# A two-layer decoder trunk on one core: early products, weight sums by DMA and one shared pool

## The chip, the cores and the metric

The kernel runs on one core of a Trainium2 chip. A core has TensorE (PE, matmuls into PSUM banks), VectorE (DVE), ScalarE (ACT), GpSimd (POOL) and SyncE (SP), and 16 DMA engines that are fed by queues; SP issues the loads here, POOL the transfers that add. The metric is the device time of one execution in microseconds (us), lower is better. A profile is taken of one execution.

## The reference

Two layers over `x` of 1 x 512 x 1024, all in fp32. The first mixer is attention beside a short convolution, the second a gated MLP over chunks of tokens; the change is in the last two lines of each layer and in what lies around them.

```python
for i in range(DEPTH):                       # 2 layers
    h = rms_norm(x, norm_g[i, 0])
    ...                                      # mix = mixer(h) @ w_out
    x = x + rms_norm(mix, norm_g[i, 1])
    h = rms_norm(x, norm_g[i, 2])
    f = (jax.nn.silu(h @ w_gate[i]) * (h @ w_up[i])) @ w_down[i]   # 1024 -> 2816 -> 1024
    x = x + rms_norm(f, norm_g[i, 3])
```

## The kernel before, in words

**Arithmetic.** An fp32 operand is split into a high and a low part (`split` for weights: a copy on ACT, L137, and a difference on DVE, L138), and each product is three matmuls: high by high, low by high, high by low. Weights are loaded raw into one of three buffers (`rawp`, 1 MB each, by SP, L310), split into pieces of 128 x 1024, and a raw buffer comes free when all its pieces and sums have been read.

**FFN.** Tokens are four tiles t0 to t3 of 128; "first tokens" are t0 and t1, "last tokens" t2 and t3. The 2816 hidden columns are 11 units of 256. A unit's gate and up products form a 2 x 2 block product (two halves of the 1024 inputs, `a` and `b`, two halves of the unit's columns, two halves of the tokens) that is done in seven products instead of eight (a scheme of the Strassen-Winograd kind). `product` (L647) is one of them: 24 matmuls of 128 x 256. Products 1, 2 and 4 take plain weights; 5, 6, 7 and 3 take the sums s1 to s4 of weights, made on DVE (`Unit.sum`, L250) and then split like the rest. On the tokens' side `Combined` makes seven operands (`hThi`, `hTlo`, L418 and L419) out of the transposed tiles, some of them differences (L424). Results go from PSUM through a copy on ACT (L727), an addition on DVE (L722), Silu on ACT (L732) and a product on DVE (L733).

**Before the FFN.** `out_proj` (L111) ends tile after tile: the last four pairs of weight rows are held back, and their products run per tile, so that t0 to t3 close one after another. Each closed tile goes through `PostNorm` (squares on ACT L497, scale on DVE L503, a root on DVE L452 and POOL L337, a Newton step L343 to L346, the sum with x L520), `pre_norm` (squares L459, h on DVE L471) and transposes on PE (L481), and then `Combined.fill`. TensorE has to have something to do in that time: the early products of the first two units, which are of the first tokens.

**The down projection** uses the same scheme (`Down`, `down_proj`), with its four sums of weights made by DMA: `sums` (L187) copies quarters of `w_down` to DRAM buffers (`tsum`) and adds others onto them, on POOL's software queue. One such DMA is issued behind each POOL instruction `pace` (L748), which reads a hidden tile and so comes when that tile is done.

**Order.** The program's order within each engine is set by a planner: `Clock` counts planned nanoseconds (`beat` for each matmul), `after` puts a step that many planned ns later, and `take` splits the weights up to three pieces ahead of the product that is next. In each layer 24 sum DMAs are issued.

## Time and profile before

| | |
|---|---|
| median of 3 runs | 1083.93 us (1079.1 to 1088.13) |
| profiled execution | 1085.33 us |
| its span in the profile | 1083.6 us |
| mean granted TensorE clock | 0.98 of full |
| TensorE busy | 1043.0 us |
| VectorE, ScalarE, GpSimd busy | 813.1, 552.5, 140.9 us |
| DMA packets | 97549, 174.79 MB |

The span is the time between the first and the last recorded event of the core; the profiled execution's own time is 1.73 us longer. Busy times are sums over instructions of an engine. The chain of waits follows the end of the program back from releaser to releaser. In the two layers, the stretch in which `out_proj` ends and the FFN begins lies at about 213 to 272 and 705 to 765 us, the units of the FFN follow to about 430 and 925 us, the end of layer 0's down projection and the start of layer 1 are at about 547 to 602 us.

### The profile page before, as it was taken

How to read it: one execution, taken by the hardware profiler on the slowest of the kernel's cores; microseconds unless marked ns; L12 is line 12 of the kernel's file. 1: busy time of each engine (PE TensorE's matmuls, PEld its weight loads, DVE VectorE, ACT ScalarE, POOL GpSimd, SP SyncE). 2: the span in 40 equal slices, each digit the busy share in tenths (PEclk: the TensorE clock that was granted, in tenths of full speed). 3: DMA queues.
4: the chain of work that ended last, by engine and by line, in shares of the span. 5: the costliest groups of instructions: out<-in, count | busy, mean ns of one | idle time of the engine just before them, and what ended most of it. 6: DMA issues, size and time to landing. Idle time of an engine off the chain costs nothing.

```text
span 1083.6 us, 16071 instructions
## 1 busy us (share of the span) xinstructions
PE 1043.0 (96%) x6395; PEld 931.7 (86%) x6395; DVE 813.1 (75%) x1179; ACT 552.5 (51%) x903; POOL 140.9 (13%) x163
## 2 busy tenths in 40 slices
PE   7999999988999899999999999997999999999997
PEld 6777778878999899998877788877999999998885
DVE  4566564588896786889978454769897787789993
ACT  4466553255643553566846333445564455455771
POOL 0011220010042131200000000010033122110000
PEclk8999999988999999999999999998999999999999
DMA  8321322312479797775727332401359889774751
GB/s 305 105 83 41 116 70 86 117 39 79 148 247 194 250 259 235 182 221 186 255 90 253 98 117 78 156 1 59 117 193 271 236 236 266 204 218 139 244 200 59
DMA packets 97549, 174.79 MB, mean 161 GB/s; under 512 B 3857, under 2 KB 64414, under 8 KB 94402
## 3 DMA queue, kind: packets, MB, share of 16 engines
q1 hardware_dynamic: 83906, 127.63, 35.6%
q0 software_dynamic: 13568, 46.14, 17.2%
q8 instruction: 50, 0.82, 0.3%
q14 instruction: 25, 0.20, 0.1%
HBM read 171.65 MB, written 48.24 MB: 203 GB/s over the span
## 4 chain that ended last, share of the span: by engine, by line
PE 76%; DVE 12%; ACT 4%; DMA 3%; issue 2%; POOL 1%; SPq 0%; POOLq 0%; DVEq 0%; ACTq 0%
PE ps L111 39%; PE ps L647 34%; DVE wlo L138 3%; DMA raw<-in_w_up_dram 2%; DVE wsum L250 1%; POOL s L337 1%; DVE h L471 1%; DVE hTlo L419 1%; ACT j L459 1%; ACT whi L137 1%; DVE x L520 1%; DMA raw<-in_w_in_even_dram 1%; PE ps L924 1%; DVE t L424 1%; PE ps L1110 1%
## 5 line engine op out<-in xcount | busy, mean ns | idle before, releaser
L647 PE MATMUL ps<-hThi,whi 128*128 128x256 f32 x1232 | 279.5, 290 | 12.7 <-ACT hThi L418 7.4
L647 PE MATMUL ps<-hThi,wlo 128*128 128x256 f32 x1232 | 278.1, 287 | 0.0
L647 PE MATMUL ps<-hTlo,whi 128*128 128x256 f32 x1232 | 277.6, 287 | 0.4 <-DVE hTlo L419 0.4
L138 DVE TENSOR_TENSOR wlo<-raw,whi 128x1024 fp32r<-128x1024 f32 (+1 forms) x206 | 239.7, 1186 | 38.1 <-ACT whi L137 37.7
L137 ACT CAST whi<-raw 128x1024 fp32r<-128x1024 f32 (+1 forms) x206 | 203.6, 1018 | 39.6 <-PE ps L647 12.4
L647 PEld LDWEIGHTS ps<-hThi,whi 128*128 128x128 f32 x1232 | 208.2, 197 | 15.6 <-ACT hThi L418 8.5
L647 PEld LDWEIGHTS ps<-hTlo,whi 128*128 128x128 f32 x1232 | 207.7, 196 | 0.9 <-DVE hTlo L419 0.9
L647 PEld LDWEIGHTS ps<-hThi,wlo 128*128 128x128 f32 x1232 | 208.4, 196 | 0.0
L111 PE MATMUL ps<-whi,whi 128*128 128x512 f32 x308 | 120.2, 391 | 2.5 <-DVE t L687 2.5
L137 ACT CAST whi<-wsum 128x1024 fp32r<-128x1024 f32 x88 | 90.2, 1045 | 60.2 <-DVE wsum L250 38.6
L138 DVE TENSOR_TENSOR wlo<-wsum,whi 128x1024 fp32r<-128x1024 f32 x88 | 105.8, 1221 | 19.8 <-ACT whi L137 19.4
L111 PE MATMUL ps<-whi,wlo 128*128 128x512 f32 x308 | 120.0, 390 | 0.0
L111 PE MATMUL ps<-wlo,whi 128*128 128x512 f32 x308 | 119.9, 389 | 0.0
L337 POOL TENSOR_TENSOR s<-s,neg_half 128x1 f32<-128x1 f32 (+1 forms) x40 | 27.5, 688 | 523.0 <-DVE s L452 446.8
L748 POOL TENSOR_SCALAR pace<-a 128x1 f32<-128x1 f32 x48 | 48.8, 1018 | 295.8 <-DVE a L733 287.8
L727 ACT COPY t<-ps 128x512 f32<-128x512 f32 x70 | 40.8, 583 | 86.9 <-PE ps L647 86.5
L722 DVE TENSOR_TENSOR t<-ps,t 128x512 f32<-128x512 f32 x88 | 58.5, 686 | 35.3 <-ACT t L727 18.4
L111 PE MATMUL ps<-whi,a 128*128 128x512 f32 x256 | 80.0, 391 | 0.0
L732 ACT ACTIVATE t<-t 128x256 f32<-128x256 f32 x88 | 36.7, 418 | 71.0 <-DVE t L722 70.9
L111 PEld LDWEIGHTS ps<-whi,whi 128*128 128x128 f32 x308 | 57.8, 188 | 15.8 <-issue 3.2
L111 PEld LDWEIGHTS ps<-wlo,whi 128*128 128x128 f32 x308 | 57.8, 188 | 12.1
L111 PEld LDWEIGHTS ps<-whi,wlo 128*128 128x128 f32 x308 | 57.8, 188 | 11.7
(143 smaller groups left out, 1470.8 us busy)
## 6 DMA issues: line engine op xcount, KB each, us to landing
tsum<-in_w_down_dram POOLq DMA_DIRECT2D x24, 1024.0 KB, 8.6
raw<-in_w_gate_dram SPq DMA_DIRECT2D x44, 512.0 KB, 4.1
raw<-in_w_up_dram SPq DMA_DIRECT2D x44, 512.0 KB, 6.2
raw<-tsum SPq DMA_DIRECT2D x16, 1024.0 KB, 5.0
raw<-in_w_down_dram SPq DMA_DIRECT2D x12, 1024.0 KB, 6.2
raw<-in_w_in_even_dram SPq DMA_DIRECT2D x10, 1024.0 KB, 6.6
tsum<-in_w_down_dram POOLq DMA_DIRECT2D x12, 768.0 KB, 7.7
tsum<-tsum POOLq DMA_DIRECT2D x8, 1024.0 KB, 9.5
```

The lines of the kernel that those rows point to most:

```text
L111: nc.tensor.matmul(out, lhsT, rhs, start=start, stop=stop, **kw)
L137: nc.scalar.copy(out=hi, in_=src)
L138: nc.vector.tensor_tensor(out=lo, in0=src, in1=hi.bitcast(F32), op=ALU.subtract)
L250: nc.vector.tensor_tensor(out=t, in0=x, in1=y, op=op)
L337: nc.gpsimd.tensor_tensor(out=y0[:, :n], in0=a, in1=neg_half[:, :n], op=ALU.pow)
L419: nc.vector.tensor_tensor(out=lo, in0=src, in1=hi.bitcast(F32), op=ALU.subtract)
L424: minus = lambda out, x, y: nc.vector.tensor_tensor(out=out, in0=x, in1=y, op=ALU.subtract)
L647: nc.tensor.matmul(bank[:, m * 256:(m + 1) * 256], piece[a][:, m, k, :], hT.at(b, p)[:, k, :], start=first and m == 0 and i == 0, stop=i = ...
L722: nc.vector.tensor_tensor(out=c, in0=x, in1=y, op=ALU.add)
L727: nc.scalar.copy(out=c, in_=x)
L732: nc.scalar.activation(out=c[:, 0:256], in_=c[:, 0:256], func=AF.Silu)
L748: nc.gpsimd.tensor_scalar(out=pace, in0=at[:, 0:1], scalar1=1.0, scalar2=None, op0=ALU.mult)
```

## The change

- The two pools for row vectors and rows (two tiles each) go; the pool `ap` of weights and activations has 39 tiles instead of 35 and serves all.
- Three units instead of two have early products. They were 7 and 3 of each, and of the next unit's product 1; they are now products 1 and 2, whose weights are plain. First and last tokens change their roles in the scheme, so that 1 and 2 are of the first tokens; the five other products of these units (5, 6, 4, 7, 3) come once all tiles are turned. For the early products a quarter of the unit's weights is loaded by itself (`plan_first`, 128 columns, in runs of 512 bytes), and for the five others the unit's weights are loaded whole again.
- `Combined.fill` gives a first tile two operands instead of two others and makes a last tile's five operands in five steps, 1400 planned ns apart.
- The sum DMAs are of two units instead of four: 48 for each layer. Each stands behind a `pace` that reads the newest temporary tile (`latest`) and is issued after products 1, 2, 4, 5 and 3.
- `out_proj` holds five pairs back instead of four; the norms of layer 1's first two tiles stand 9000 planned ns later.

`L647` of before is L679 of the changed kernel, L137/L138 are L135/L136, L250 is L263, L418/L419/L424 are L429/L432/L438, L459/L471/L481 are L491/L503/L513, L497 is L529, L722/L727/L733 are L754/L759/L765, L337 is L344, L187 is L186.

ScalarE, at the end of layer 0's `out_proj` (`t` a temporary tile, `j` a throwaway output of the squares), before:

```order
L418 CAST hThi_2093<-t_2183 128x4x128
L418 CAST hThi_2097<-ps_2175 128x4x128
L459 ACTIVATE j_2143,s_2142<-x_91 128x512
L459 ACTIVATE j_2145,s_2142<-x_91 128x512
L727 COPY t_2262<-ps_2213 128x512
L497 ACTIVATE j_2196,s_2195<-ps_1788 128x512
L137 CAST whi_2270<-wsum_2268 128x1024
L497 ACTIVATE j_2198,s_2195<-ps_1789 128x512
L418 CAST hThi_2307<-ps_2297 128x4x128
```

and now:

```order
L529 ACTIVATE j_2184,s_2183<-ps_1782 128x512
L529 ACTIVATE j_2186,s_2183<-ps_1783 128x512
L135 CAST whi_2201<-raw_1935 128x1024
L491 ACTIVATE j_2235,s_2234<-x_86 128x512
L759 COPY t_2249<-ps_2199 128x512
L491 ACTIVATE j_2237,s_2234<-x_86 128x512
L135 CAST whi_2251<-raw_2010 128x1024
L429 CAST hThi_2277<-t_2270 128x4x128
L429 CAST hThi_2280<-t_2271 128x4x128
```

Before, the copy L727 of an early product stands ahead of the squares L497 of t3; now the squares (L529) are first, and the copy L759 is behind them.

VectorE in the same place (`wsum` a weight sum, `s` the norm's small vectors, `h` the normed row of t2), before:

```order
L138 TENSOR_TENSOR wlo_2218<-wsum_2215,whi_2217 128x1024
L452 SCALAR_TENSOR_TENSOR s_2147<-s_2142,eps_t 128x1
L250 TENSOR_TENSOR wsum_2264<-raw_1892,raw_2122 128x1024
L343 TENSOR_TENSOR s_2161<-s_2149 128x1
L250 TENSOR_TENSOR wsum_2266<-wsum_2264,raw_1892 128x1024
L344 SCALAR_TENSOR_TENSOR s_2162<-s_2161,s_2147 128x1
L250 TENSOR_TENSOR wsum_2268<-raw_2122,wsum_2266 128x1024
L346 SCALAR_TENSOR_TENSOR s_2163<-s_2162,s_2149 128x1
L471 SCALAR_TENSOR_TENSOR h_2167<-x_91,s_2163,g_1780 128x512 x2
```

and now, in the stretch that makes the last operands ahead of product 5 (`a` at L765 is a hidden tile):

```order
L432 TENSOR_TENSOR hTlo_2278<-t_2270,hThi_2277 128x4x128
L765 TENSOR_TENSOR a_2323<-t_2320 128x256
L438 TENSOR_TENSOR t_2403<-ps_2393,a_2149 128x512
L136 TENSOR_TENSOR wlo_2328<-raw_2106,whi_2327 128x1024
L432 TENSOR_TENSOR hTlo_2281<-t_2271,hThi_2280 128x4x128
L432 TENSOR_TENSOR hTlo_2308<-t_2273,hThi_2307 128x4x128
L432 TENSOR_TENSOR hTlo_2340<-ps_2265,hThi_2339 128x4x128
L263 TENSOR_TENSOR wsum_2370<-raw_2205,raw_2255 128x1024
L438 TENSOR_TENSOR t_2404<-ps_2398,t_2403 128x512
L754 TENSOR_TENSOR t_2422<-ps_2326,t_2368 128x512
L136 TENSOR_TENSOR wlo_2373<-wsum_2370,whi_2372 128x1024
L263 TENSOR_TENSOR wsum_2376<-wsum_2370,raw_2205 128x1024
```

Before, three weight sums (L250) and a split stand between the norm's steps and h; now the first weight sum of the program, `wsum_2370`, stands behind the operands `hTlo` of the last tokens.

GpSimd, near the program's start (`tsum` are the DRAM sums), before:

```order
L337 TENSOR_TENSOR s_149<-s_147,neg_half 128x1
L337 TENSOR_TENSOR s_195<-s_193,neg_half 128x1
L337 TENSOR_TENSOR s_258<-s_256,neg_half 128x1
```

and now:

```order
L344 TENSOR_TENSOR s_143<-s_141,neg_half 128x1
L186 DMA tsum_75<-in_w_down_dram 128x2x512
L186 DMA tsum_79<-in_w_down_dram 128x2x512
L344 TENSOR_TENSOR s_189<-s_187,neg_half 128x1
```

Before, POOL has no DMA among the first norm's powers; now the first sum DMA of each layer, 512 KB each, stands right behind the first of them.

The diff:

```diff
-    ap_ = pool("ap", 35)
-    gp = pool("gp", 2)
-    hp = pool("hp", 2)
+    ap_ = pool("ap", 39)
...
-    EARLY = 2
+    EARLY = 3
...
+        PAIRS = [slice(u, min(u + 2, UNITS)) for u in range(0, UNITS, 2)]
...
-                    for g in self.GROUPS
+                    for g in self.PAIRS
...
+        SOON_EARLY = {5: ["s2"], 6: ["s3"], 4: ["s4"]}
...
+        def plan_first(self):
+
+            for p, ks in ((1, slice(0, 4)), (2, slice(4, 8))):
+                plan((self, p), self.chunk(ks, slice(0, P)), ALL)
+            self.READS = {k: v for k, v in self.READS.items() if k not in (1, 2)}
+            self.SOON = self.SOON_EARLY
+
+        def plan_rest(self, products):
             for name, ks in (("a", slice(0, 4)), ("b", slice(4, 8))):
-                self.half[name] = Chunk([P, 2, 4, 256], [((ALL, m), v[:, ks, :])
-                                                         for m, v in enumerate(ws)])
+                self.half[name] = self.chunk(ks, slice(0, 256))
             for names in self.READS.values():
                 for n in names:
                     self.half[n].left += 1
-            self.sums = {}
+            for p in products:
+                self.plan(p)
...
-    FIRST, THEN, STEADY = (7, 3), (1, 2, 4, 6, 5), (1, 2, 4, 6, 5, 7, 3)
+    THEN, STEADY = (5, 6, 4, 7, 3), (1, 2, 4, 6, 5, 7, 3)
 
     def plan_ffn(layer):
         units = [Unit(layer, c * 256) for c in range(UNITS)]
-        early, done = units[:EARLY], []
-        for i, u in enumerate(early):
-            for p in FIRST + ((1,) if i + 1 < EARLY else ()):
-                u.plan(p)
-        for i, u in enumerate(early):
-            for p in THEN[1 if i + 1 < EARLY else 0:]:
-                u.plan(p)
-        for u in units[EARLY:]:
-            for p in STEADY:
-                u.plan(p)
+        for u in units[:EARLY]:
+            u.plan_first()
+        for i, u in enumerate(units):
+            u.plan_rest(THEN if i < EARLY else STEADY)
...
             if t < 2:
                 kept = act([P, 2, 512])
-                e1, e2 = (quad(kept[:, i, :]) for i in range(2))
-                nc.scalar.copy(out=e1, in_=b1)
-                nc.scalar.copy(out=e2, in_=b2)
-                self.kept[t] = (e1, e2)
-                d = quad(tmp())
-                minus(d, b2, e1)
-                self.put(7, t, d)
-                self.put(3, t, b2)
-            else:
-                e1, e2 = self.kept[t - 2]
+                self.kept[t] = [quad(kept[:, i, :]) for i in range(2)]
                 self.put(1, t, b1)
-                t1, t2, t4 = (quad(tmp()) for _ in range(3))
-                minus(t1, e1, b1)
-                minus(t2, e2, t1)
                 self.put(2, t, b2)
-                minus(t4, b2, t2)
-                self.put(4, t, t4)
-                self.put(6, t, t2)
-                self.put(5, t, t1)
-            self.n_turned += 1
+                for e, b in zip(self.kept[t], (b1, b2)):
+                    nc.scalar.copy(out=e, in_=b)
+                self.n_turned += 1
+                return
+            e1, e2 = self.kept[t - 2]
+            t1, t2, t3, t4, l2 = (quad(tmp()) for _ in range(5))
+
+            def one():
+                minus(t1, b1, e1)
+                minus(t2, b2, t1)
+                self.high(5, t, t1)
+                self.high(6, t, t2)
+
+            def two():
+                self.low(5, t, t1)
+                minus(t4, e2, t2)
+                self.high(4, t, t4)
+                nc.scalar.copy(out=l2, in_=b2)
+
+            def three():
+                self.low(6, t, t2)
+                self.low(4, t, t4)
+                self.high(3, t, b2)
+
+            def four():
+                minus(t3, l2, b1)
+                self.low(3, t, b2)
+                self.high(7, t, t3)
+
+            def five():
+                self.low(7, t, t3)
+                self.n_turned += 1
+
+            for i, step in enumerate((one, two, three, four, five)):
+                clock.after(1400 * i, step)
...
+            c = latest[0] = tmp()
...
-            if i >= EARLY and (f, half) != (1, FIRST_TOKENS):
-                sum_on(hidden.at(f, half, i))
...
         def run(bank, u, p, first=True, more=3):
             product(bank, p, take(more, (u, p)), hT, first, layer == 0)
+            if hT.n_turned == NT and p not in (6, 7):
+                sum_on(latest[0])
...
-        kept = ExitStack()
-        kept.enter_context(tc.manual_schedule(engines={mybir.EngineType.Pool}))
-        for u in units[:EARLY]:
-            r, z = psum(), psum()
-            run(r, u, 7)
-            p7 = copied(r)
-            run(z, u, 3)
-            early.append((r, z, p7))
-        clock.until(lambda: hT.n_turned == NT)
-        for i, u in enumerate(units):
+        for i, u in enumerate(units[:EARLY]):
             x, y = psum(), psum()
             run(x, u, 1)
             a = copied(x)
             run(y, u, 2)
-            finish(plus(y, a), 0, LAST_TOKENS, i)
+            finish(plus(y, a), 0, FIRST_TOKENS, i)
+            early.append(x)
+        clock.until(lambda: hT.n_turned == NT)
+        kept = ExitStack()
+        kept.enter_context(tc.manual_schedule(engines={mybir.EngineType.Pool}))
+        for i, u in enumerate(units):
             if i < EARLY:
-                r, z, p7 = early[i]
-                run(r, u, 4, False)
+                x, q, w = early[i], psum(), psum()
+                run(q, u, 5)
                 run(x, u, 6, False)
                 u2 = copied(x)
-                finish(plus(r, u2), 1, LAST_TOKENS, i)
-                run(x, u, 5, False)
-                v = copied(x)
-                finish(plus(z, v), 0, FIRST_TOKENS, i)
-                finish(plus(x, p7), 1, FIRST_TOKENS, i)
+                run(w, u, 4)
             else:
+                x, y = psum(), psum()
+                run(x, u, 1)
+                a = copied(x)
+                run(y, u, 2)
+                finish(plus(y, a), 0, FIRST_TOKENS, i)
                 w, q = psum(), psum()
                 run(w, u, 4)
                 run(x, u, 6, False)
                 u2 = copied(x)
                 run(q, u, 5)
-                run(x, u, 7, False)
-                u3 = copied(x)
-                finish(plus(w, u3), 1, LAST_TOKENS, i)
-                finish(plus(q, u3), 1, FIRST_TOKENS, i)
-                run(q, u, 3, False)
-                finish(plus(q, u2), 0, FIRST_TOKENS, i)
+            run(x, u, 7, False)
+            u3 = copied(x)
+            finish(plus(w, u3), 1, FIRST_TOKENS, i)
+            finish(plus(q, u3), 1, LAST_TOKENS, i)
+            run(q, u, 3, False)
+            finish(plus(q, u2), 0, LAST_TOKENS, i)
...
-    out_proj(Mixed([mixed[k] for k in MIX_ORDER]), 4, g_post,
+    out_proj(Mixed([mixed[k] for k in MIX_ORDER]), 5, g_post,
...
-        pre_norm(t, g_pre1, hT1[0], WAITS)
+        clock.after(9000 if t < 2 else 0, lambda: pre_norm(t, g_pre1, hT1[0], WAITS))
```


## Rows read from the trace of the kernel before

**Rows 1.** The page's first part: busy us, share and instructions by engine.

```profile
PE 1043.0 (96%) x6395; PEld 931.7 (86%) x6395; DVE 813.1 (75%) x1179; ACT 552.5 (51%) x903; POOL 140.9 (13%) x163
```

**Rows 2.** By stage: stretch, length, busy us by engine, clock, DMA share, GB/s.

```profile
180.00:200.00 20.00, 20.00 (x90) 16.57 (x89) 12.96 (x14) 8.10 (x9) 0.00 (x0) 1.00 0.57 182
...
300.00:320.00 20.00, 20.00 (x169) 20.00 (x168) 18.88 (x22) 10.78 (x16) 11.03 (x8) 1.00 0.70 238
...
231.50:241.50 10.00, 6.33 (x28) 6.13 (x29) 9.53 (x17) 3.59 (x9) 1.39 (x1) 0.66 0.35 107
...
250.70:262.00 11.30, 7.89 (x38) 7.05 (x38) 10.51 (x19) 7.70 (x13) 0.54 (x1) 0.70 0.28 83
...
722.00:732.50 10.50, 8.50 (x46) 6.93 (x44) 8.72 (x18) 6.71 (x15) 1.09 (x2) 1.00 0.02 3
...
732.50:741.50 9.00, 7.31 (x40) 7.31 (x41) 8.49 (x17) 4.67 (x11) 1.44 (x1) 0.62 0.37 115
...
741.50:753.00 11.50, 7.97 (x67) 7.72 (x67) 10.61 (x23) 6.16 (x13) 1.09 (x2) 1.00 0.16 47
...
753.00:763.00 10.00, 9.99 (x70) 9.68 (x71) 10.00 (x15) 7.12 (x10) 0.00 (x0) 0.83 0.33 106
...
360.00:380.00 20.00, 17.02 (x132) 16.82 (x131) 15.17 (x18) 8.49 (x12) 3.06 (x5) 0.91 0.71 258
...
860.00:880.00 20.00, 17.93 (x137) 17.72 (x137) 16.30 (x19) 10.51 (x14) 3.44 (x5) 0.91 0.76 272
```

**Rows 3.** TensorE's waits, 215 to 290 us, with what ended them.

```profile
PE ps L647 <- ACT hThi L418: 3.7, 1, 3.7
...
PE ps L481 <- DVE h L471: 3.0, 1, 3.0
```

**Rows 4.** Timeline of ScalarE at 241 us: start, us, engine, line, operation, idle before.

```profile
241.46 0.59 ACT L727 COPY t<-ps 128x512 f32<-128x512 f32 x1 [4.49 <-PE ps L647]
...
241.94 0.60 ACT L497 ACTIVATE j<-ps 128x512 bf16<-128x512 f32 x1
```

**Rows 5.** Timeline of VectorE, 252 to 259 us.

```profile
252.99 1.41 DVE L471 SCALAR_TENSOR_TENSOR h<-x,s,g 128x512 f32<-128x512 f32 x2
...
254.32 1.28 DVE L419 TENSOR_TENSOR hTlo<-t,hThi 128x512 fp32r<-128x512 f32 x2
...
256.12 0.68 DVE L424 TENSOR_TENSOR t<-a,ps 128x512 f32<-128x512 f32 x1
...
256.72 2.35 DVE L138 TENSOR_TENSOR wlo<-raw,whi 128x1024 fp32r<-128x1024 f32 x2
...
258.99 0.69 DVE L424 TENSOR_TENSOR t<-a,t 128x512 f32<-128x512 f32 x1
```

**Rows 6.** Chain of waits, 340 to 375 us: start, us, what.

```profile
352.90 0.37 SPq L310
...
353.31 11.40 DMA raw<-in_w_up_dram
```

**Rows 7.** Timeline of GpSimd, 350 to 416 us.

```profile
354.51 0.21 POOL L748 TENSOR_SCALAR pace<-a 128x1 f32<-128x1 f32 x1 [3.40 <-DVE a L733]
...
359.27 1.04 POOL L748 TENSOR_SCALAR pace<-a 128x1 f32<-128x1 f32 x1 [3.40 <-DVE a L733]
...
403.22 1.04 POOL L748 TENSOR_SCALAR pace<-a 128x1 f32<-128x1 f32 x1 [1.82 <-DVE a L733]
...
412.56 0.88 POOL L187 DMA_DIRECT2D tsum<-tsum  x1 [8.30 <-issue]
```

**Rows 8.** Timeline of TensorE at 569 us.

```profile
569.80 0.47 PE L111 MATMUL ps<-whi,whi 128*128 128x512 f32 x1 [2.26 <-DVE t L687]
```

**Rows 9.** By stage: two stretches of the handover, and the first 20 us.

```profile
547.00:585.00 38.00, 35.07 (x161) 28.30 (x160) 30.21 (x56) 21.48 (x40) 3.12 (x5) 1.00 0.38 133
...
585.00:602.00 17.00, 14.69 (x71) 11.48 (x70) 12.10 (x31) 9.43 (x25) 2.02 (x3) 1.00 0.49 165
...
0.00:20.00 20.00, 13.96 (x50) 10.89 (x51) 8.38 (x18) 9.23 (x17) 1.99 (x11) 0.74 0.89 307
```

More of the change, by code (lines that the diff above doesn't have):

```diff
@@ L100, in trunk @@
     small = lambda n: sp.tile([P, n], F32, tag="s", name=nm("s"), padded_shape=[P, 4])
-    row_tile = lambda: hp.tile([P, D], F32, tag="h", name=nm("h"))
+    row_tile = lambda: ap_.tile([P, D], F32, tag="a", name=nm("h"))
     pair = lambda: ap_.tile([P, 2, 512], F32R, tag="a", name=nm("a"))
@@ L209, in trunk, with chunk @@
         SOON = {2: ["s1"], 4: ["s3", "s2"], 6: ["s4"]}
+        SOON_EARLY = {5: ["s2"], 6: ["s3"], 4: ["s4"]}
         def __init__(self, layer, c0):
-            ws = [col_chunk(w[layer], c0, 256) for w in (w_gate, w_up)]
-            self.half = {}
+            self.ws = [col_chunk(w[layer], c0, 256) for w in (w_gate, w_up)]
+            self.half, self.sums = {}, {}
+        def chunk(self, ks, cols):
+            return Chunk([P, 2, 4, cols.stop - cols.start],
+                         [((ALL, m), w[:, ks, cols]) for m, w in enumerate(self.ws)])
+        def plan_first(self):
[4 more added lines that the diff above has]
+        def plan_rest(self, products):
             for name, ks in (("a", slice(0, 4)), ("b", slice(4, 8))):
-                self.half[name] = Chunk([P, 2, 4, 256], [((ALL, m), v[:, ks, :])
-                                                         for m, v in enumerate(ws)])
+                self.half[name] = self.chunk(ks, slice(0, 256))
             for names in self.READS.values():
@@ L350, in row_vector @@
     def row_vector(v):
-        t = gp.tile([P, D], F32, tag="g", name=nm("g"))
+        t = ap_.tile([P, D], F32, tag="a", name=nm("g"))
         nc.sync.dma_start(out=t, in_=v.partition_broadcast(P))
@@ L412, in put, with part @@
         def put(self, p, t, src):
+            self.high(p, t, src)
+            self.low(p, t, src)
+        def part(self, a, p, t):
             if p not in self.tiles:
@@ L415, in put, with high, low @@
                                  for n in ("hThi", "hTlo")]
-            cs = slice((t % 2) * P, (t % 2) * P + P)
-            hi, lo = (x[:, :, cs] for x in self.tiles[p])
-            nc.scalar.copy(out=hi, in_=src)
-            nc.vector.tensor_tensor(out=lo, in0=src, in1=hi.bitcast(F32), op=ALU.subtract)
+            return self.tiles[p][a][:, :, (t % 2) * P:(t % 2) * P + P]
+        def high(self, p, t, src):
+            nc.scalar.copy(out=self.part(0, p, t), in_=src)
+        def low(self, p, t, src):
+            nc.vector.tensor_tensor(out=self.part(1, p, t), in0=src,
+                                    in1=self.part(0, p, t).bitcast(F32), op=ALU.subtract)
         def fill(self, t, banks):
@@ L717, in ffn @@
     def ffn(layer, units, hT, g_post, then, next_ahead, store=False):
-        hidden = Hidden()
+        hidden, latest = Hidden(), [None]
         def plus(x, y):
-            c = tmp()
+            c = latest[0] = tmp()
             nc.vector.tensor_tensor(out=c, in0=x, in1=y, op=ALU.add)
@@ L725, in copied @@
         def copied(x):
-            c = tmp()
+            c = latest[0] = tmp()
             nc.scalar.copy(out=c, in_=x)
@@ L1136, in trunk @@
     hT = Combined()
-    out_proj(Mixed(mixed), 4, g_post, lambda t: pre_norm(t, g_pre, hT, WAITS), (1, 2, 3))
+    out_proj(Mixed(mixed), 5, g_post, lambda t: pre_norm(t, g_pre, hT, WAITS), (1, 2, 3))
     g_post = row_vector(norm_g[1, 3])
```

2 lines of the change are left out of this document (1 added, 1 removed).

## The prediction

> **What bounds the kernel now.** First the page's busy times: TensorE works 1043.0 of a span of 1083.6 us [rows 1], so the whole of what can be won without taking matmuls away is what it stands still or runs slowly. The change takes no matmul away: the seven products of eleven units stay. Next the table by stage [rows 2] shows where it does so. At full clock 20 us hold 90 matmuls 128x512 (0.222 us each) or 169 of 128x256 (0.118 us each); a stretch with fewer has lost the difference. In the first stretch after layer 0's `out_proj` 28 matmuls fill 10.0 us, at a granted clock of 0.66, which is a mixture of the two levels of 1.2 and 2.4 GHz: 10.0 − 28 × 0.118 = 6.7 us lost. From 250.7 us there are 38 (transposes counted at the same price) in 11.3 us: 6.8 lost. Layer 1 spreads the same over four stretches: 2.0 (10.50 − 8.50, all idle, since the clock there is 1.00), 4.3 (9.0 − 40 × 0.118), 3.5 (11.50 − 7.97) and 1.7 (10.0 − 70 × 0.118). Both transitions together lose 25.0 us. The wait table says with what each begins: 3.7 us on ScalarE's `hThi`, 3.0 on VectorE's h [rows 3]. The reader should note that a stop of 3 to 4 us costs about twice its length, because the clock is low behind it.
>
> Two later stretches, 360 to 380 and 860 to 880 us, hold 132 and 137 matmuls in place of 169 [rows 2]: 4.4 and 3.8 us lost, 8.2 together. The chain of waits there goes through one raw load of `w_up` that takes 11.40 us to land [rows 6]. The handover between the layers is idle for 2.9 + 2.3 = 5.2 us at full clock [rows 9], of which one wait on `down_proj`'s VectorE addition is 2.26 [rows 8]. In sum 38 us are in places that the change touches.
>
> **The change, part by part.**
>
> *Early products 1 and 2 of three units.* Before, the early products needed a weight sum and a split of it ahead of them; VectorE had three sums and a split between the norm's small steps and h of t2, and ScalarE the copy of a product ahead of t3's squares (it began at 241.46, the squares only at 241.94, having waited 4.49 us for that product [rows 4]). Both go. The early work of TensorE is now six products of 24 × 0.118 = 2.83 us and needs none of the tiles that are late. I laid the new order out by hand at pitches of the trace: 0.60 for a VectorE operation of 512 (256.12 to 256.72), 1.14 for a split (2.27 for two), 1.33 for h of one tile [rows 5]. By this no gap is left where `out_proj` ends: the first operand is ready some 2 us before. With E for that end, h of t2 is done at about E + 2.6.
>
> VectorE is next late. From there to the last operand of product 5, the first that needs the last tokens, stand 16 operations of 512 (9.6), 6 splits (6.8), two of the pairs at 1.33 (2.7) and ten small ones, together an estimated 2.0: 21.1, so ready at E + 23.7. TensorE has 6 × 2.83 = 17.0 of products, 16 transposes at 0.118 = 1.9, and a stop for h of t3 that was 3.0 and has less in front of it now; nothing bounds it but 0 and 3.0, and I take 1.3. It arrives at E + 20.2 and waits 3.5. Behind it, another 11.4 us of VectorE work stand ahead of the operands of products 6 and 4, for which TensorE has less work: some 1.9 more. A stop of that length has been followed by a low clock; at a low clock TensorE needs its operands later, so part of it replaces the second stop, and I add 1.0 net, between 0 and the 3.0 that the first stop of before cost beyond its own 3.7. Left over: 1.3 + 3.5 + 1.9 + 1.0 = 7.7 in layer 0; in layer 1, whose product takes the low parts of the tokens last within a bank, I take 7.0. Gain: 25.0 − 14.7 = **10.3**. The third early unit then keeps VectorE at some 13 us for each unit of five products against TensorE's 5 × 2.83 = 14.2, so TensorE bounds again.
>
> *Sum DMAs halved, spread and begun earlier.* Before, 24 in each layer come only from unit 2 on, and crowd the stretch where the raw load takes 11.40 us. Its raw buffer is asked for no earlier now: VectorE's order around the units is the same. What changes is what the load shares the queues with: an add of 512 KB in place of one of 1 MB, and earlier units take part. The weights are read twice for three units, some 3 MB per layer more. The bounds are 0 (the load as late as now) and all of the 8.2; a half of an add goes, so I take the middle, **4.5**.
>
> *Quarter loads.* They land in the time of `out_proj`, whose stretches move 1 GB/s and later 107 at a DMA share of 0.35 or less [rows 2]; hidden, 0. If they were late, the first product would wait up to one landing, and the 11.40 of [rows 6] is the worst one.
>
> *Later norms, five pairs held.* The norms of layer 1's first tiles move behind the VectorE addition on which TensorE waited 2.26, and the shorter waits after it. Bounds 0 and 5.2; I take **2.0**, most of that one wait. Holding one more pair only regroups `out_proj`'s matmuls: 0.
>
> *Two DMAs at the start.* The first sum of each layer, 512 KB each, now goes out behind the first power. The first 20 us run at a DMA share of 0.89 with 307 GB/s, and TensorE is busy 13.96 of them [rows 9]: 1 MB more in front of loads that are awaited costs at most 1.05 MB / 307 GB/s = 3.4, or nothing if they share later. I take −**0.7**, since the issues come when most loads of the start are already queued.
>
> *The smaller pieces.* `pace` reads a temporary tile and costs 0.21 or 1.04 us on GpSimd [rows 7], which has 140.9 of 1083.6 us to do [rows 1]: 0. The sums are needed by the down projection after the last unit, so that their pace decides nothing there.
>
> Sum: 10.3 + 4.5 + 2.0 − 0.7 = 16.1. Against the profiled execution, 1085.3 − 16.1 = **1069 us**. That execution is 1.4 above the median of the runs, so that the median could come out a little lower; I leave that in the range.
>
> **The rivals.**
>
> *A. VectorE is late nowhere.* If the planner's spacing of `fill` holds and splits come in TensorE's shadow, the transitions lose only the 1.3 twice and the DMA stall goes: 1085.3 − (25.0 − 2.6) − 8.2 − 2.0 = 1053, at best, with all 38 us, 1047. For it: before, VectorE is busy 9.53 of 10.0 us there only because sums stand in it [rows 2]. Against it: nine operations more in `fill` for each last tile.
>
> *B. Given back at product 5.* Stops of 3.5 and more each take a low clock with them, as before at about twice their length: 3.5 + 1.9 + 1.3 becomes 13 per layer, all of the 25 but nothing of the DMA stall is won, or the stall stays because the two hoisted DMAs are the only ones that really moved. Then 1085.3 + 0.7 − 2.0 − 0 to 8 = 1076 to 1084. For it: VectorE was busy 18.88 of 20 us in the units before [rows 2], so it has nothing to catch up with.
>
> *C. Slower, by POOL's queue.* `pace` holds a temporary tile until POOL reaches it, and POOL waits for its own adds: behind the `pace` of 403.22 the next DMA went out only at 412.56 after 8.30 us [rows 7]. There are eight temporary tiles, some seven are used in a unit of 19.9 us, so one is wanted again after about 22.7 us. If POOL falls more than that behind, ScalarE's copies stop, and TensorE with them. Half of the 48 DMAs of a layer are adds on what a previous one wrote; if only 24 of these 48 in the kernel cost 1 us of that kind, 1085.3 − 16.1 + 24 = **1093**. It decides when POOL's backlog is longer than 22.7 us. Against it: an add of half the size, and five places per 19.9 us.
>
> *D. GpSimd and VectorE shut each other out.* The `pace` instructions now fall into the early units too, nine in each layer, where I have VectorE late. A `pace` of 1.04 in place of 0.21 [rows 7] shows that something holds it; if VectorE were held as long in its turn, 18 × 0.21 to 18 × 1.04 = 4 to 19 us come back, 1073 to 1088. The Trainium skill, page "SBUF — State Buffer", section "Who interferes with whom", says that a VectorE instruction with two inputs in SBUF and a GpSimd instruction that reads SBUF exclude each other for the whole instruction. The trace bears out only that GpSimd's side is lengthened: the splits beside keep their pitch of 1.14 [rows 5]. So this gets a small chance.
>
> **How the numbers follow.** Forecast 0.46, A 0.20, B 0.22, C 0.05, D 0.07. The predicted time is the forecast's, 1069; its own bounds are 1062 (all of the DMA stall and of the handover won, 3.7 and 3.2 more) to 1080 (nothing of either won, and the clock at 3.0 in each layer). The range leaves out the best end of A, C and the ends of D: 1050 to 1083. About 1% is what a measurement of this kernel can tell from no change, 1073 to 1095. Faster by more than that: A and most of the forecast (0.40), 0.60. Within it: B, D and the rest of the forecast, 0.34. Slower needs C's full price or several of the bounds at once: 0.06.
>
> **What would show it.** In the changed trace no wait of TensorE on ScalarE where `out_proj` ends, and no clock below 1.00 in the 10 us behind it. A stop of about 3.5 us on VectorE's `hTlo` (L432) some 20 us later, which is the weakest step: 0 there speaks for A, over 5 for B. The raw load of unit 6 landing in less than 8 us, and more than 150 matmuls in 20 us there. The wait of 2.26 on the down projection's addition under 1. A first wait for raw data, at about 10 us, that is longer by less than a microsecond. A ScalarE copy or VectorE addition that waits on POOL would show C. The forecast is wrong if TensorE's losses in the two transitions stay above 20 us or fall below 8.

## The result, and the profile after

The changed kernel takes 1069.77 us (median of 4, 1069.21 to 1071.01) against 1082.22 of the kernel before (4 runs, 1079.1 to 1088.13): a ratio of 0.988, 95% interval 0.9834 to 0.9926. The profiled execution took 1071.01 us with a span of 1069.1; before it was 1085.33 and 1083.6, so the two traces differ by 14.5. One execution of the later kernel "sums late" (1261.1 us, granted clock 0.75) ran in a slower state and is in no median below.

The page's first part, where [rows 1] had 1043.0 and 813.1: TensorE's busy time fell by 8.5 us with the same 6395 matmuls, and the rest of the 14.5 is less idle time. Most of the 8.5 should be slow clock: the mean granted clock rose from 0.98 to 0.99. It can't be told exactly, since busy time also grows where matmuls stop and start (21.20 us for seven products at a clock of 1.00 below, where 20.16 is full rate).

```profile
PE 1034.5 (97%) x6395; PEld 923.1 (86%) x6395; DVE 812.6 (76%) x1179; ACT 552.1 (52%) x903; POOL 191.4 (18%) x259
```

By stage (columns as in [rows 2]): the 10 and 11.5 us behind `out_proj` in layer 0, the handover (FFN's end shifted by 3.2, the stretch 547 to 585 of [rows 9]), and the seven products in a row in which each layer had its DMA stop.

```profile
231.50:241.50 10.00, 10.00 (x80) 9.73 (x79) 8.96 (x21) 7.40 (x19) 1.26 (x3) 1.00 0.53 156
241.50:253.00 11.50, 10.18 (x85) 9.74 (x84) 11.50 (x20) 7.84 (x14) 0.36 (x1) 1.00 0.84 255
543.80:579.00 35.20, 35.20 (x164) 29.18 (x163) 28.68 (x57) 18.29 (x39) 3.12 (x5) 1.00 0.36 118
348.75:368.91 20.16, 20.16 (x170) 20.16 (x169) 18.69 (x22) 10.67 (x15) 7.33 (x9) 1.00 0.84 208
835.52:855.68 20.16, 20.16 (x171) 20.16 (x170) 18.69 (x22) 10.64 (x15) 7.54 (x9) 1.00 0.86 210
```

Where 28 matmuls stood at a clock of 0.66 there are now 80 instructions at 1.00. The handover's 35.2 us hold 164 instructions without idle time, where 38 held 161, and the groups of seven products that took 23.65 and 22.50 us before take 20.16.

But the gain behind `out_proj` is largely given back. The same table, bounded by TensorE's first product and its 29th (28 products and 16 transposes; at full rate seven products take 20.16 us, so this is 4 × 20.16 + 16 × 0.118 = 82.5). First the kernel before:

```profile
235.17:328.42 93.25, 89.69 (x689) 88.11 (x690) 83.80 (x113) 52.47 (x82) 15.21 (x11) 0.93 0.48 156
734.19:825.59 91.40, 87.79 (x689) 86.70 (x689) 83.63 (x113) 52.28 (x82) 18.10 (x11) 0.95 0.45 147
```

Then the changed one, with the second and third seven of layer 0 and the second of layer 1:

```profile
233.05:328.44 95.39, 86.74 (x689) 84.44 (x688) 86.15 (x116) 51.85 (x80) 24.66 (x31) 0.98 0.75 208
259.60:283.34 23.74, 21.20 (x171) 20.39 (x170) 21.83 (x27) 11.56 (x17) 9.17 (x11) 1.00 0.71 209
283.34:306.73 23.39, 20.73 (x171) 20.33 (x169) 19.53 (x24) 11.30 (x16) 6.00 (x6) 1.00 0.91 237
...
722.34:815.26 92.92, 84.98 (x689) 82.84 (x688) 86.14 (x115) 52.09 (x80) 25.19 (x31) 1.00 0.72 205
748.06:772.47 24.41, 21.18 (x171) 20.37 (x169) 21.74 (x27) 11.56 (x17) 8.96 (x11) 1.00 0.67 201
```

From the start of `out_proj`'s last matmul to that of the first product it was 4.09 and 4.08 us before, and is 0.23 in both layers. The 28 products behind it take 2.1 and 1.5 us more than before, although the clock is better. The first seven, with all the transposes, is not what got longer (VectorE is busy nearly all of it):

```profile
233.05:259.60 26.55, 23.11 (x186) 22.07 (x185) 25.57 (x46) 17.48 (x31) 1.62 (x3) 1.00 0.53 160
722.34:748.06 25.72, 22.69 (x186) 21.97 (x185) 24.59 (x45) 17.72 (x31) 1.65 (x3) 1.00 0.45 144
```

It took 32.11 and 30.10 us before. What the 28 wait for in layer 0 (233 to 330 us; us in all, times, longest) is many short things; the last line is SP, whose loads wait for VectorE's weight sums:

```profile
PE ps L679 <- DVE wlo L136: 2.8, 4, 0.9
PE ps L679 <- ACT whi L135: 2.2, 2, 1.8
PE ps L679 <- DVE t L754: 1.8, 1, 1.8
PE ps L513 <- DVE h L503: 1.3, 1, 1.3
PE ps L679 <- DVE hTlo L432: 0.5, 1, 0.5
...
SPq L317 <- DVE wsum L263: 47.3, 8, 13.4
```

The chain of waits there alternates between VectorE and a load: VectorE's weight sum reads a buffer's last quarter, only then SP issues the next load, VectorE's split of it is late, and so on. No split waits for a free tile of the pool in these stretches of either layer.

```profile
290.81 1.14 DVE wsum L263
291.94 0.35 DVE a L765
292.29 0.05 SPq L317
...
292.38 8.17 DMA raw<-in_w_up_dram
...
300.63 1.06 ACT whi L135
...
303.99 1.22 DVE wlo L136
305.21 1.21 DVE t L754 x2
...
306.46 23.58 PE ps L679 x181
```

The whole account, before less after, from starts of matmuls in the two traces: end of layer 0's `out_proj` 231.08 to 232.82, −1.7; stops ahead of the first products +7.7; first 28 products −2.1 and −1.5; the products behind them +3.2 and +4.5 (the DMA stops); layer 0's last product to the end of layer 1's `out_proj`, 252.7 to 247.9, +4.8; the tail −0.4. Sum 14.5.

### The profile page after: what moved, and what is told of

Its sections match the earlier page's. It is cut to its first block, busy times and chain, and to the rows that moved or that the text cites. A ratio compares the mean times of both kernels' runs of the same rounds, so it can differ in the third digit from the quotient of the medians.

```text
span 1069.1 us, 16311 instructions
## 1 busy us (share of the span) xinstructions
PE 1034.5 (97%) x6395; PEld 923.1 (86%) x6395; DVE 812.6 (76%) x1179; ACT 552.1 (52%) x903; POOL 191.4 (18%) x259
## 4 chain that ended last, share of the span: by engine, by line
PE 72%; DVE 15%; DMA 4%; ACT 3%; issue 3%; POOL 1%; SPq 0%; DVEq 0%; POOLq 0%; ACTq 0%
PE ps L109 41%; PE ps L679 28%; DVE wlo L136 5%; DMA raw<-in_w_up_dram 3%; DVE wsum L263 3%; ACT whi L135 1%; POOL s L344 1%; DVE hTlo L432 1%; DVE h L503 1%; DVE t L754 1%; ACT j L491 1%; DVE x L552 1%; PE ps L952 1%; DMA raw<-in_w_in_even_dram 1%; DVE t L438 1%
## 5 line engine op out<-in xcount | busy, mean ns | idle before, releaser
L679 PE MATMUL ps<-hThi,whi 128*128 128x256 f32 x1232 | 275.1, 285 | 8.2 <-ACT whi L135 4.9
L679 PE MATMUL ps<-hThi,wlo 128*128 128x256 f32 x1232 | 275.0, 284 | 5.1 <-DVE wlo L136 5.1
L679 PE MATMUL ps<-hTlo,whi 128*128 128x256 f32 x1232 | 274.0, 284 | 1.3 <-DVE hTlo L432 1.3
L136 DVE TENSOR_TENSOR wlo<-raw,whi 128x1024 fp32r<-128x1024 f32 (+1 forms) x206 | 239.7, 1185 | 31.7 <-ACT whi L135 30.7
L135 ACT CAST whi<-raw 128x1024 fp32r<-128x1024 f32 (+1 forms) x206 | 203.6, 1018 | 27.3 <-DMA raw<-in_w_up_dram 7.8
L679 PEld LDWEIGHTS ps<-hThi,whi 128*128 128x128 f32 x1232 | 203.6, 192 | 10.6 <-ACT whi L135 5.9
L679 PEld LDWEIGHTS ps<-hThi,wlo 128*128 128x128 f32 x1232 | 204.0, 192 | 6.6 <-DVE wlo L136 6.5
L679 PEld LDWEIGHTS ps<-hTlo,whi 128*128 128x128 f32 x1232 | 203.8, 192 | 1.9 <-DVE hTlo L432 1.9
L135 ACT CAST whi<-wsum 128x1024 fp32r<-128x1024 f32 x88 | 90.1, 1045 | 57.7 <-DVE wsum L263 50.4
L779 POOL TENSOR_SCALAR pace<-t 128x1 f32<-128x1 f32 x96 | 74.2, 773 | 245.9 <-ACT t L764 172.4
L136 DVE TENSOR_TENSOR wlo<-wsum,whi 128x1024 fp32r<-128x1024 f32 x88 | 105.5, 1219 | 15.9 <-ACT whi L135 15.9
L344 POOL TENSOR_TENSOR s<-s,neg_half 128x1 f32<-128x1 f32 (+1 forms) x40 | 25.0, 627 | 486.8 <-DVE s L484 415.2
L754 DVE TENSOR_TENSOR t<-ps,t 128x512 f32<-128x512 f32 x88 | 58.4, 684 | 32.8 <-ACT t L759 17.6
L759 ACT COPY t<-ps 128x512 f32<-128x512 f32 x66 | 38.5, 583 | 86.2 <-PE ps L679 86.2
L186 POOL DMA_DIRECT2D tsum<-in_w_down_dram x72 | 68.4, 953 | 2.1 <-issue 0.8
```

The source lines that it names most:

```text
L135: nc.scalar.copy(out=hi, in_=src)
L136: nc.vector.tensor_tensor(out=lo, in0=src, in1=hi.bitcast(F32), op=ALU.subtract)
L186: return [lambda to=to, of=of, g=g, op=op: nc.gpsimd.dma_start(out=to[:, g, :], in_=of[:, g, :], accum_op=op) for g in self.PAIRS for op, ...
L344: nc.gpsimd.tensor_tensor(out=y0[:, :n], in0=a, in1=neg_half[:, :n], op=ALU.pow)
L679: nc.tensor.matmul(bank[:, m * 256:(m + 1) * 256], piece[a][:, m, k, :], hT.at(b, p)[:, k, :], start=first and m == 0 and i == 0, stop=i = ...
L754: nc.vector.tensor_tensor(out=c, in0=x, in1=y, op=ALU.add)
```

## The experiments

All ratios below are of runs against the kernel before on the same chip. The kernel before has medians of 1082.2 to 1084.0 there, so two medians of different kernels that are less than 2 us apart tell little. "Sevens" are seven products in a row, counted from each layer's first; at full rate one takes 20.16 us. The kernels without low parts leave out part of the arithmetic: the high part of a weight stands in for its low part, in the early units alone.

| kernel | us | ratio to before, interval | first 28, layers 0 and 1 | 2nd and 3rd seven, layer 0; layer 1 |
|---|---|---|---|---|
| before | | | 93.3, 91.4 | 20.8, 20.2; 20.8, 20.3 |
| changed | 1069.8 | 0.988 (0.983 to 0.993) | 95.4, 92.9 | 23.7, 23.4; 24.4, 21.8 |
| no hoist | 1069.3 | 0.989 (0.986 to 0.993) | 94.3, 93.0 | 22.3, 23.7; 24.4, 21.8 |
| no delay | 1074.6 | 0.995 (0.992 to 0.998) | 95.5, 92.9 | 23.7, 23.8; 24.4, 21.8 |
| sums late | 1074.4 | 0.995 (0.991 to 0.998) | 92.1, 92.1 | 22.4, 21.0; 24.4, 21.8 |
| no low parts | 1066.0 | 0.986 (0.982 to 0.989) | 93.0, 91.5 | 20.8, 20.6; 20.3, 21.8 |
| four raw buffers | 1064.3 | 0.982 (0.979 to 0.985) | 91.6, 92.0 | 22.3, 21.0; 24.4, 21.7 |
| four, and no low parts | 1054.8 | 0.976 (0.973 to 0.978) | 88.4, 85.7 | 20.8, 20.2; 20.3, 20.2 |
| four, and GpSimd | 1069.6 | 0.990 (0.987 to 0.992) | 93.6, 94.4 | 25.6, 21.0; 24.2, 21.7 |
| two early units | 1074.6 | 0.991 (0.987 to 0.994) | 97.8, 94.8 | 20.7, 20.2; 20.5, 20.3 |
| fill at once | 1076.4 | 0.995 (0.993 to 0.997) | 99.3, 94.9 | 25.1, 26.9; 23.7, 24.5 |
| 1 MB sums | 1072.6 | 0.991 (0.987 to 0.995) | 95.2, 94.5 | 23.8, 23.2; 24.4, 21.8 |
| before + delay | 1079.8 | 0.996 (0.993 to 0.998) | 92.4, 92.3 | 20.8, 20.2; 20.8, 20.3 |
| before + sums | 1077.5 | 0.994 (0.992 to 0.997) | 92.4, 94.2 | 20.8, 20.2; 20.8, 23.0 |

**No hoist.**

```diff
         early = []
+        kept = ExitStack()
+        kept.enter_context(tc.manual_schedule(engines={mybir.EngineType.Pool}))
...
-        kept = ExitStack()
-        kept.enter_context(tc.manual_schedule(engines={mybir.EngineType.Pool}))
```

> The changed kernel, with POOL's order written out from the first early product on, so that no sum DMA is ahead of the FFN. If the two hoisted DMAs cost the start its 1.74 us (out_proj ended at 232.82 in place of 231.08 although the rest of the first layer's mixer kept its pace), out_proj ends at about 231.1 again and the time is about 1068.0, 1.7 less than the changed kernel. Rival: the 1.74 is chance of that one execution (the clock at the start was low for 13.65 us, before for 10.24) or comes from another edit: time within 0.5 of the changed kernel's 1069.8.

Within 0.5 us: the rival's outcome. Its `out_proj` ended at 232.0. The traces show no cost of the hoisted DMAs. On the chip that ran this kernel it ended at 231.8 and 232.5 with the two DMAs ahead of it (no delay, no low parts) and at 232.0 and 231.8 without (this kernel and sums late, which moves them too). On another chip it ended at 231.8 with them (four raw buffers) and at 232.0 to 232.3 without (two early units and the two kernels made from the one before). On a third chip, where every kernel had them, it ended at 233.0 to 235.1. The granted clock of the first 40 us differs from execution to execution, 0.79 to 0.91. The 1.74 is therefore no measure of a cost.

**The delay, taken out of the changed kernel and put alone into the kernel before.**

```diff
-        clock.after(9000 if t < 2 else 0, lambda: pre_norm(t, g_pre1, hT1[0], WAITS))
+        pre_norm(t, g_pre1, hT1[0], WAITS)
```

> The changed kernel without the 9000 planned ns ahead of the norms of layer 1's first two tiles. If this delay is what shortened the stretch from layer 0's last FFN product to the end of layer 1's out_proj from 252.7 to 247.9 us, the wait on down_proj's VectorE addition is back at 2 us or more and the stretch is 252 to 253, the time about 1074.5. Rival: the stretch is shorter by the five held pairs or by the new roles of the tokens: it stays under 249, time 1070 to 1071.

> The kernel before with nothing but the 9000 planned ns ahead of the norms of layer 1's first two tiles. If the delay alone is what shortened the handover: the stretch from layer 0's last FFN product to the end of layer 1's out_proj falls from 252.7 to about 248, time about 4.8 under the kernel before. Rival: 252 to 253, no change.

The stretch is 251.9 us without the delay and 247.4 with it alone; 4.9 us of the changed kernel's time hang on it, and 4.3 are won by it in the kernel before (its interval allows 1.7 to 7.3). Shown from both sides: the handover is the delay's. One expectation missed: without the delay no wait on the down projection's addition comes back. TensorE waits 2.5 us on h, 0.9 on a split and 0.8 on `hThi` instead, where the kernel before waited 2.7 on h and 2.3 on the addition, and the changed one 1.2 on h. So the delay saves the stretch, whichever wait stands in it. The trace of before with the delay also has no DMA stop in layer 0, though its sums are untouched:

```profile
360.00:380.00 20.00, 20.00 (x169) 20.00 (x168) 18.99 (x22) 11.02 (x15) 5.12 (x8) 1.00 0.84 304
```

So the stop of 4.4 us in [rows 2] is not in every execution of those sums. This execution took 1074.7 us, 5.0 below the median of its kernel.

**Sums: halved and spread alone; spread but not halved; kept out of the early units.**

In the kernel before, with the changed kernel's places and its latest tile:

```diff
-                    for g in self.GROUPS
+                    for g in self.PAIRS
```

In the changed kernel the reverse, at every second place; and, as another kernel, the places moved:

```diff
-                    for g in self.PAIRS
+                    for g in self.GROUPS
```

```diff
-            if hT.n_turned == NT and p not in (6, 7):
+            if u not in units[:EARLY]:
```

> The kernel before with nothing but the sum DMAs of 512 KB, issued behind products 1, 2, 4, 5 and 3 from the turned tiles on. If halving and spreading them is what took the stop at unit 5 (units of 23.65 and 22.50 us at full-rate 20.16, and 21.2 and 21.7 behind them): these four units fall to 20.2 to 20.5, time about 7 to 8 under the kernel before. Rival (the stop went because the units arrive there in another phase, or VectorE's order): the 2 to 3.5 us stay somewhere in units 4 to 8.

> The changed kernel with sum DMAs of four units (1 MB, 24 in a layer) behind every second of its places, so spread but not halved. If halving matters, a raw load behind a 1 MB add lands late as before: a unit of 22 us or more in both layers, time 1072 to 1075. If spreading alone does it, units 4 to 10 stay at 20.2 to 21.4 and the time within 1 of 1069.8.

> The changed kernel with no sum DMA in the three early units; the 48 of a layer come behind every product of the eight units after them. In the changed kernel the early units (first to 28th product) take 95.4 us in layer 0 and 92.9 in layer 1 against 82.5 of matmuls and transposes. Theory L (raw loads are late, since sum DMAs share the queues with them): they fall to about 88 and 87; the later units get denser traffic and may lose up to 5 of it, time 1064 to 1070. Theory V (VectorE's own work in the early units): they stay within 1.5 of 95.4 and 92.9, time 1070 to 1075.

With small sums alone the sevens of the old stop take 20.16 in both layers and the time falls by 6.5 us (interval 3.5 to 8.8). The load of `w_up` on which the old stop hung, 11.40 us in [rows 6], lands in 5.1 there (8.0 in the trace with the delay alone, which has no stop either). But a seven of 23.0 came earlier, in layer 1, and the chain goes through another late load there:

```profile
782.11 11.74 DMA raw<-in_w_up_dram
```

In the changed kernel the loads do not land sooner on the whole. Those of `w_up` issued from 340 to 425 us (count, size, median us to landing of those whose landing is recorded), before and then changed:

```profile
raw<-in_w_up_dram SPq DMA_DIRECT2D x8, 512.0 KB, 9.3
```

```profile
raw<-in_w_up_dram SPq DMA_DIRECT2D x8, 512.0 KB, 10.0
```

So what is shown is that the stop went with the new sums, not that smaller sums make every load faster. With 1 MB sums the sevens from the fifth to the tenth take 20.2 to 21.1; its 2.9 us over the changed kernel are partly its start (`out_proj` ended at 234.5), and the intervals overlap, so halving and spreading are not told apart. Late sums: layer 0's early stretch falls by 3.3, layer 1's by 0.9, neither theory's figure, and later sevens of 22.75 and 24.4 us take it back; its executions scatter from 1070.3 to 1086.2. The traffic of the sums is a part of the early loss in layer 0 (the third and fourth seven fall from 45.1 together to 41.2) and none of the 24.4 in layer 1.

**VectorE's work, and the buffers.**

In `split`, for products 5, 6, 4, 7 and 3 of the early units; and, as another kernel, the pools (`load` then allows four); and both:

```diff
+        if not with_lo:
+            return hi, hi
```

```diff
-    rawp = pool("rawp", 3)
+    rawp = pool("rawp", 4)
-    ap_ = pool("ap", 39)
+    ap_ = pool("ap", 37)
```

> The changed kernel without the low parts of the weights for the five later products of the early units: the high part stands in for them, so that 15 VectorE operations of 1.14 us (17 us) are missing in each layer. Theory V: the early units fall from 95.4 and 92.9 to under 87 in both layers, time about 1053 to 1058. Theory L: VectorE waits for the loads instead; early units 91 to 94 and 89 to 92, time 1065 to 1069.

> The changed kernel with four raw buffers in place of three, and 37 tiles in the pool for all in place of 39. Theory L in the form that a buffer comes free too late (a load is issued only when VectorE has read the last quarter out of a buffer): early units fall from 95.4 and 92.9 to about 88 and 86, time 1056 to 1062. Theory V: early units within 1.5 of what they were, time 1068 to 1071. With 37 tiles, operations could wait for a tile, which would show as slower than 1071.

> Four raw buffers and, for the five later products of the early units, no low parts of the weights (the high part stands in). Four buffers alone took layer 0's units 1 and 2 from 23.74 and 23.39 to 22.28 and 21.00 us but left layer 1's at 24.41 and 21.73; no low parts alone took them to 20.79 and 20.58, and 20.31 and 21.78, but pushed the next unit to 24.5. If VectorE binds first and the loads behind it, both together leave neither: units 1 to 3 at 20.2 to 20.8 in both layers, first 28 products 87 to 89 us, time 1054 to 1057. If the unit of 24.5 in the run without low parts has another cause than the buffers, it stays and the time is 1060 or more.

Each alone helps where the other doesn't. Without low parts the second seven runs without a stop in both layers, but the fourth takes 24.5 us:

```profile
259.83:280.62 20.79, 20.79 (x169) 20.69 (x169) 14.89 (x19) 11.80 (x18) 6.78 (x10) 0.97 0.87 251
...
301.20:325.73 24.53, 21.99 (x171) 21.75 (x169) 18.98 (x24) 9.54 (x15) 7.75 (x11) 0.93 0.95 271
```

With a fourth buffer layer 0's third and fourth are mended, as they were by late sums, and layer 1's second is what it was, to a hundredth:

```profile
282.28:303.28 21.00, 20.41 (x171) 20.21 (x169) 19.82 (x24) 11.44 (x16) 9.38 (x7) 1.00 0.88 220
303.28:323.59 20.31, 20.31 (x170) 20.21 (x169) 18.84 (x22) 11.33 (x16) 7.91 (x11) 1.00 1.03 299
...
741.89:766.30 24.41, 21.17 (x170) 20.36 (x169) 21.74 (x27) 11.57 (x17) 8.93 (x11) 1.00 0.67 201
```

The 22.3 of layer 0's second seven with four buffers is no gain: its first takes 28.0 for 26.6, and both together 50.3 in either kernel. The stop at product 5 is the same (1.83 us on ScalarE's split), but a low clock follows it in one trace and not in the other. Ten microseconds behind it, in the changed kernel and then with four buffers:

```profile
256.40:266.40 10.00, 9.30 (x71) 8.70 (x71) 10.00 (x14) 6.38 (x11) 2.94 (x3) 1.00 0.50 158
```

```profile
255.40:265.40 10.00, 9.86 (x67) 9.66 (x68) 10.00 (x14) 6.39 (x11) 3.00 (x3) 0.83 0.50 157
```

VectorE is busy all of the ten in both, so that the slower TensorE cost nothing there: VectorE is the bound. With both changes the second to fourth sevens are at 20.2 to 20.8:

```profile
233.23:321.59 88.36, 85.10 (x690) 84.04 (x688) 72.97 (x104) 52.58 (x80) 22.70 (x31) 0.98 0.85 242
...
714.18:799.86 85.68, 83.47 (x690) 82.55 (x689) 72.81 (x104) 53.08 (x80) 22.32 (x31) 1.00 0.84 238
```

Single gains of 3.8 (low parts) and 5.5 us (buffers) become 14.9 together: two bounds in a row. Where VectorE's work is taken away the loads bind one unit later, and the gain is given back in the fourth seven. Layer 1's third seven shows it best: 21.8 and 21.7 with either change alone, 20.2 with both. Four buffers alone is a whole kernel, and at 1064.3 us the fastest one of this study that leaves nothing of the reference out.

**Work moved to GpSimd.**

```diff
-                self.low(6, t, t2)
+                self.low(6, t, t2, nc.gpsimd)
```

The same for products 4 and 7, in the kernel with four raw buffers.

> Four raw buffers, and three of a last tile's five low parts (of products 6, 4 and 7) made by GpSimd in place of VectorE: six operations of 0.60 us less on VectorE in each layer's early stretch. If VectorE's share of the work is what is left there: layer 1's unit 1 falls from 24.41 by 2 to 3 us, layer 0's unit 1 from 22.28 by 1 to 2, time 1059 to 1062. If GpSimd and VectorE exclude each other, or GpSimd takes over 2 us for each: hTlo is late at products 6 and 4, unit 0 and 1 longer, time 1065 to 1070.

The rival's outcome: 5.4 us slower than four buffers alone (of which the first 28 products show 2.0 and 2.4). By lines, 235 to 300 us of layer 0 (busy us, mean ns; idle before), first this kernel, then four buffers alone:

```profile
L432 POOL TENSOR_TENSOR hTlo<-t,hThi 128x512 fp32r<-128x512 f32 x6 | 11.3, 1888 | 11.1 <-ACT hThi L429 11.1
```

```profile
L263 DVE TENSOR_TENSOR wsum<-raw,wsum 128x1024 f32<-128x1024 f32 x3 | 4.7, 1582 | 0.0
L263 DVE TENSOR_TENSOR wsum<-raw 128x1024 f32<-128x1024 f32 x3 | 4.7, 1582 | 0.0
```

```profile
L263 DVE TENSOR_TENSOR wsum<-raw 128x1024 f32<-128x1024 f32 x3 | 3.6, 1217 | 0.0
L263 DVE TENSOR_TENSOR wsum<-raw,wsum 128x1024 f32<-128x1024 f32 x3 | 3.6, 1215 | 0.0
```

Six operations of 0.60 left VectorE, and two groups of its weight sums grew from 1216 to 1582 ns on average. (GpSimd's line is from 225 to 330 us, since it holds all six.) The averages hide that one of each three is held and the others are not. In the timeline the two long ones stand beside a `hTlo` of GpSimd:

```profile
261.50 2.31 DVE L263 TENSOR_TENSOR wsum<-raw 128x1024 f32<-128x1024 f32 x1
...
265.46 2.31 DVE L263 TENSOR_TENSOR wsum<-raw,wsum 128x1024 f32<-128x1024 f32 x1
```

```profile
260.92 1.81 POOL L432 TENSOR_TENSOR hTlo<-t,hThi 128x512 fp32r<-128x512 f32 x1 [3.90 <-ACT hThi L429]
...
265.14 1.55 POOL L432 TENSOR_TENSOR hTlo<-t,hThi 128x512 fp32r<-128x512 f32 x1 [1.24 <-ACT hThi L429]
```

GpSimd ends at 262.73 and 266.69, VectorE 1.08 us later each time, about what a sum takes undisturbed: VectorE's operation stood until GpSimd's was over.

**Fewer early units, and the fill not spaced.**

```diff
-    EARLY = 3
+    EARLY = 2
```

```diff
-                clock.after(1400 * i, step)
+                clock.after(0, step)
```

> The changed kernel with two early units in place of three. TensorE then has four products (11.3 us) in place of six between the transposes, so it reaches product 5 some 5.7 us sooner and must wait for VectorE's last operand there: a stop of about 6 to 8 us less what VectorE saves (two splits, one addition: 3.5), so 4 to 6, with a low clock behind it; but one unit less is read twice and comes as five products. If the loss is at product 5: time 1073 to 1078. If the loss is a price of each early unit (about 3 us each): time 1064 to 1069.

> The changed kernel with the five steps of a last tile's operands planned all at once in place of 1400 planned ns apart. If the spacing is what keeps the stop at product 5 at 2.8 us: VectorE makes all nine operands of t2 ahead of the splits and of t3's norm, TensorE waits 3 us or more before t3's transposes or at product 5 with a low clock behind it, time 1072 to 1076. Rival: the order hardly matters, since VectorE has the same sum of work before product 5: 1069 to 1071.

With two units TensorE stops at product 5, as the first branch had it, but for 7.1 us in place of 4 to 6 (4.2 and 3.0), and the clock falls; in 245 to 265 us VectorE is never idle:

```profile
PE ps L679 <- ACT hThi L429: 4.4, 2, 4.2
PE ps L679 <- DVE hTlo L432: 3.0, 1, 3.0
PE ps L513 <- DVE h L503: 2.7, 1, 2.7
```

```profile
245.00:265.00 20.00, 10.69 (x50) 9.90 (x51) 20.00 (x30) 10.15 (x17) 5.38 (x2) 0.66 0.44 131
```

Its later sevens run nearly at full rate, so the loss moves: it is paid in one long stop at product 5, or in stops behind the third early unit. Without the spacing TensorE waits 3.4 us before the last transposes and 3.6 for a split in the third seven; 1076.4 us is at the end of what was expected (1072 to 1076). This edit also moves six sum DMAs in place of two to the start, and `out_proj` ended at 235.1, so the loss need not all be the spacing's.

## Why the prediction was right, and where it was not

The total came out at 1069.8 for 1069, but by terms that missed in both directions, and that they cancel is luck. The forecast was taken from the profiled execution of before: against it the profiled execution of the changed kernel is 14.3 us shorter, for 16.1, and the medians differ by 12.5. The forecast called itself wrong if the two transitions lost over 20 us or under 8. Counted to the end of the second seven they lose 16.0 (before 27.1); counted to the 28th product they lose 23.3 (95.4 and 92.9, less 82.5 each; before 27.3), which is over its limit. Both figures of before include the 7.7 ahead of the first products.

*Early products.* Right: no gap where `out_proj` ends, clock 1.00 for 20 us, a stop before t3's transposes of 1.3 as taken. At product 5 TensorE lost 2.8 us in three pieces, 20.8 us after its first product, where 3.5 at E + 20.2 were forecast; but the longest piece ended on ScalarE's split of a weight sum, not on `hTlo`, and no low clock followed. To the end of the second seven the layers lose 8.1 and 7.9 us, close to the 7.7 and 7.0 of the forecast.

*The step that failed* is "the third early unit then keeps VectorE at some 13 us for each unit of five products against TensorE's 14.2, so TensorE bounds again". The third and fourth sevens lose 4.8 and 2.5 us, where the forecast put nothing and the kernel before loses 0.2 in all. VectorE was busy 21.8 us in the second seven, since the rest of the last tiles' operands falls there too. Behind that its work would have fitted (19.5 us in layer 0's third), but the loads came behind its weight sums and its splits behind the loads. Both bounds were shown by taking them away singly and together. The transitions therefore gave 7.7 − 2.1 − 1.5 = 4.1 us, not 10.3: most of the way to rival B, in many short stops instead of a few long ones.

*Sum DMAs.* 7.7 us between the traces for 4.5. That the new sums took the stop is shown by the kernel before with these sums alone (6.5 us in medians). The size is uncertain, since the stop is not in every execution, and the forecast's reason, a smaller add ahead of the load, fits the one load of [rows 6] but not the loads of these units as a whole.

*Handover.* 4.8 for 2.0: TensorE's waits there fell from 5.0 to 1.2 us. The term was mis-sized by counting only the wait of [rows 8]; the waits for h fell as well.

*Start.* −1.7 between the traces for −0.7, but no cost of the DMAs is shown; the first wait for raw data is not longer (7.65 us, before 8.11). *Rival A* did not come about, and needed both bounds gone (1054.8, near its 1053). One argument against it was miscounted: `fill` has nine VectorE operations for a last tile where there were eight, not nine more. *Rival C*: no wait of ScalarE or VectorE on `pace` stands in the trace (those on POOL are for the norms' powers and for attention). *Rival D*: the splits of [rows 5] have no `pace` beside them, since the first one stands at 298 us, so those rows could not bear on it. The whole traces do. In the changed kernel the 75 splits of 128x1024 that ran beside a `pace` took 1218 ns on average, the 233 others 1221; before they were 1220 (25) and 1222. So the pace costs VectorE nothing here. The pair does exclude when GpSimd's operation is long (2.31 us for 1.22 above). This agrees with the Trainium skill, "SBUF — State Buffer", section "Who interferes with whom", on instructions of this kind; for the very short read of a `pace` no run shows a price on VectorE's side.

## What to carry to other kernels

When a stop is filled with work that needs no late operand, ask at once what that work's own supply costs: here weights read twice, five products per pair of loads instead of seven, and VectorE behind both. Two bounds in series hide each other, so take each away alone and then both before judging either. A total that agrees is no proof of its terms: set milestones in both traces and compare stretch by stretch.

## What the runs showed of the hardware

Executions of the kernel before spread over 1077.3 to 1088.2 us in four sets of runs, the four of the changed kernel over 1069.2 to 1071.0. The stops of 3 to 4 us that are followed by a low clock (0.66 and 0.70 in [rows 2]) are gone in the latter. That the stops make the spread is not shown: the kernel with late sums has none so long where the FFN begins, and spread over 1070.3 to 1086.2.

In the changed kernel a stop of 2.1 us at 254.3 was followed by a clock of 1.00, one of 2.0 at 304.4 by 0.92 over the next seven. The first of these stops, of the same length, was followed by 0.83 over ten microseconds with four raw buffers. The length of a stop alone did not tell what the clock would do, and where VectorE was the bound the low clock cost no time.

A VectorE addition of 128x1024 that GpSimd's subtraction of 128x512 held took 2.31 us in place of 1.22; 75 splits beside a read of 128x1 were not held at all.
